# The first layer's gate and second scale vectors on TensorE: two more modulation vectors as column-tiled products with c

## The chip, the core and the metric

The kernel runs on one core of a Trainium2 chip. The core has a matrix engine (TensorE, PE in the profile; its weight loads are listed as PEld), a vector engine (VectorE, DVE), a scalar engine for activations and copies (ScalarE, ACT), a general engine (GpSimd, POOL) and a queue from which the transfers from memory are issued (SyncE, SP). They run side by side, each through its own instructions in order, and wait for one another through semaphores. The metric is the device time of one execution in microseconds; lower is better.

## The reference

Four residual layers over 256 tokens of width 1024; the mixers are sliding-window attention, gated linear attention, forgetting attention and sliding-window attention again. Every layer has six modulation vectors, made from one conditioning vector `c`:

```python
c_act = jax.nn.silu(c)
for i in range(DEPTH):
    mod = c_act @ ada_w[i] + ada_b[i]                 # (1, 1024) @ (1024, 6144)
    sh1, sc1, g1, sh2, sc2, g2 = jnp.split(mod, 6, axis=-1)
    h = modulate(rmsnorm(x, norm_gain[i, 0]), sh1, sc1)
    y = mixer_i(h)                                    # layer 0: swa_mixer
    x = x + g1[:, None, :] * y
    h = modulate(rmsnorm(x, norm_gain[i, 1]), sh2, sc2)
    x = x + g2[:, None, :] * swiglu(h, ffn_w_gu[i], ffn_w_down[i])
return rmsnorm(x, final_norm)
```

`modulate(h, shift, scale)` is `h * (1 + scale) + shift`. The vectors are numbered 0 to 5 in the order of the split. Everything is float32. `ada_w` alone is 4 x 6 x 4 MB, and all weights are read once: 296 MB in one execution.

## The kernel before

All weights come as a stream of items of at most 1 MB, kept in order by the class `Stream`. An item is loaded into one of five `raw` buffers (`RAW = 5`) on SP's queue (`load_raw`, L181), so the load of an item waits until the item five places earlier is done with its buffer. There are two kinds of items.

A weight item ("w") is split into a high and a low part for the three-product matmul `mm3` (L277 to L279): ACT makes `wh` (L194) and DVE subtracts to make `wl` (L196), in two pieces each.

A modulation item ("a") holds the weights of 256 entries of one modulation vector. Before the change there are two ways to use it. For most vectors `ada_pieces` gives two pieces, each a DVE instruction over 128 x 1024 elements that multiplies the weights by `cact` (c after silu, on every partition) and sums (L213); it writes one column of 128 entries of `mod`. For the first two vectors of layer 0 (shift and scale of the first norm) `ada_rows` gives a product and a turn instead. The product is eight matmuls with a 32-column `ccol` as stationary operand and 256 columns of weights moving, which go to four groups of 32 columns of the array and so to four groups of partitions of one PSUM bank (L228), followed by an ACT copy to `row` (L229). The turn is two matmuls of `row` with a column of ones, which adds the four groups and turns the row into two columns (L233), and a DVE add of the bias into `mod` (L235). For these vectors the weights lie in memory by rows of `c`, 256 columns to an item (`_layout`).

In layer 0 the order of items is written out by hand in `ORDER0 = "shwshshwshwwwgwwgggSwHSwHSSHHw"`: w is the next weight item of the mixer (six input chunks i0_0 to i0_5, four output chunks o0_0 to o0_3), and s, h, g, H, S are the next item of vectors 1, 0, 2, 3, 4, four of each. The pieces of the items are put into the program between the matmuls of the chunks: `start_chunk` divides the pieces pending (up to two weight items ahead) by the eight ticks of a chunk, and each `tick` emits as many as are due. A tick comes after six matmuls of `mm3`. The same tick advances the attention, which runs as a generator (`attn_heads`) between the projections: scores (L576), masked minimum on DVE (L589), exponentials on ACT (L594), scaling (L562, L564), transposes (L617, copied at L618), the product with v (L606), and the split of the result (L510, L511). The chunks of q are rotated on DVE (L639 to L646) and transposed (L679).

`out_proj` then forces the gate (vector 2) and multiplies in two halves of the inner dimension; each output tile is added to x with the gate on DVE (L514). Before the second half `next_norm` forces vectors 3 and 4 (H and S). The PSUM tag "mm" has three banks, which hold the results of the projections; "t" has two and holds transposes, statistics and the results of `ada_rows`. The instructions of an engine don't stand strictly in program order: in the trace the attention's matmuls are found between those of a projection.

Of the kernel before, what the change touches and what calls it, by code (L numbers as in the profile page):

```python
# [17 lines left out]
P = 128  # L18
D = 1024
KT = D // P  # L20
S = 256
# [46 lines left out]
GLA_RATE = (0.585, 2.55)  # L68
FOX_RATE = (0.64, -7.0, 0.68, 1.02)
STAT = (1, 1, 1)  # L70
PSBUFS = {"mm": 3, "s": 2, "t": 2, "o": 1}


# [69 lines left out]
class Builder:  # L143
# [24 lines left out]
    def ps(self, tag):  # L168
        return self.t(self.psum, [P, 512], tag, bufs=PSBUFS[tag])

# [29 lines left out]
    def ada_pieces(self, it, raw):  # L200

        nc = self.nc
        layer, nt = it[1]
        mod = self.mod[layer]
        bias = self.c("ada_b")[:, layer * 48:(layer + 1) * 48]

        if layer == 0 and nt < 2 * KT:
            return self.ada_rows(mod[:, nt:nt + 2], bias[:, nt:nt + 2], raw)

        def piece(i):  # L210
            w = raw[:, i * D:(i + 1) * D]
            col, b = mod[:, nt + i:nt + i + 1], bias[:, nt + i:nt + i + 1]
            nc.vector.tensor_tensor_reduce(out=w, in0=w, in1=self.cact, scale=1.0, scalar=b,  # L213
                                           op0=ALU.mult, op1=ALU.add, accum_out=col)
        return [lambda: piece(0), lambda: piece(1)]

    def ada_rows(self, mod, bias, raw):


        nc = self.nc  # L220
        w = raw[:, :2048].rearrange("p (k n) -> p k n", k=KT)
        ps = self.ps("t")
        row = self.t(self.small, [P, S], "fc", bufs=2)

        def product():
            for k in range(KT):
                j = k % 4 * 32
                nc.tensor.matmul(ps[j:j + 32, :S], self.ccol[:, k], w[:, k], start=k < 4, stop=k >= 4)  # L228
            nc.scalar.copy(row, ps[:, :S])  # L229

        def turn():
            for m in range(2):
                nc.tensor.matmul(ps[:, S + m:S + m + 1], row[:, m * P:(m + 1) * P], self.c("one"),  # L233
                                 start=True, stop=True)
            nc.vector.tensor_tensor(out=mod, in0=ps[:, S:S + 2], in1=bias, op=ALU.add)  # L235
        return [product, lambda: self.turns.append(turn)]


    def start_chunk(self, ticks):
# [224 lines left out]
    def first_chunk(self, name, tok=False):  # L464
# [9 lines left out]
        for k in range(KT):  # L474
            for m in range(2):
                sl = slice(m * P, (m + 1) * P)
                first, last = k == 0, k == KT - 1
                self.mm3(outs[m][:, :S + 2], wh[:, k, sl], wl[:, k, sl], uh[:, k], ul[:, k], first, last)
            if k == STAT[0]:
                self.stat_start(self.acc)  # L480
            if k == STAT[1]:
                self.stat_end()
            if k == STAT[2]:
                nc.scalar.copy(rbs, self.spread(self.y))
# [811 lines left out]
def _chunks(w, cols):  # L1296

    k, n = w.shape
    return w.reshape(k // P, P, n // cols, cols).transpose(2, 1, 0, 3).reshape(n // cols, P, -1)


def _halves(w):

    n = w.shape[0]
    return w.reshape(n, 2, 4, P, 2, 512).transpose(0, 1, 4, 3, 2, 5).reshape(n, 4, P, 2048)


def _colmajor(v):

    return v.reshape(-1, P).T  # L1310


def _layout(i):
    f = np.float32
    a = {}
    a["x"] = i["x"][0].T.reshape(KT, P, S).transpose(1, 0, 2)
    a["c"] = i["c"].reshape(1, D)
    ada = i["ada_w"].reshape(DEPTH, D, 6, D).transpose(0, 2, 3, 1)
    a["ada"] = ada.reshape(DEPTH * 6, 4, 2, P, D).transpose(0, 1, 3, 2, 4).reshape(DEPTH * 6, 4, P, 2 * D)
    for v in range(2):  # L1320
        a["ada"][v] = _chunks(i["ada_w"][0, :, v * D:(v + 1) * D], 256)
    gu = i["ffn_w_gu"].reshape(DEPTH, KT, P, 2, FT, P)[:, :, :, :, :2]
    gu = gu.transpose(0, 4, 2, 1, 3, 5).reshape(DEPTH, 2, P, KT * 2 * P)
    gt = i["ffn_w_gu"].reshape(DEPTH, 2, KT // 2, P, 2, FT // 2, 2 * P)[:, :, :, :, :, 1:]
    gt = gt.transpose(0, 5, 1, 3, 2, 4, 6).reshape(DEPTH, FT - 2, P, KT * 2 * P)
    a["gu"] = np.concatenate([gu, gt], 1)
    dn = i["ffn_w_down"].reshape(DEPTH, 2, FT // 2, P, KT, P)
    a["down"] = dn.transpose(0, 4, 1, 3, 2, 5).reshape(DEPTH, KT, 2, P, (FT // 2) * P)

    swa = i["swa_w_in"]  # L1330
    a["swa_in"] = np.stack([_chunks(np.concatenate([w[:, 1024:], w[:, :1024]], 1), 256) for w in swa])
    a["swa_o"] = _halves(i["swa_w_o"])
    w = i["gla_w_in"][0]
    gq, gk, gv, gr, ga = np.split(w, [512, 1024, 2048, 3072], axis=1)
    a["gla_in"] = _chunks(np.concatenate(
        [gr, gq[:, :256], gk[:, :256], gq[:, 256:], gk[:, 256:], gv], 1), 256)[None]
    a["gla_va"] = _chunks(np.concatenate([gv[:, :256], ga], 1), 272)[0]
    a["gla_gate"] = i["gla_w_gate_up"][0]
    a["gla_o"] = _halves(i["gla_w_o"])
    w = i["fox_w_in"][0]  # L1340
    fq, fk, fv, ff = np.split(w, [1024, 2048, 3072], axis=1)
    a["fox_in"] = _chunks(np.concatenate(
        [t[:, 256 * g:256 * g + 256] for g in range(4) for t in (fq, fk, fv)], 1), 256)[None]
    a["fox_vf"] = _chunks(np.concatenate([fv[:, :256], ff], 1), 272)[0]
    a["fox_o"] = _halves(i["fox_w_o"])

    c, c2 = np.zeros((P, CONST_W), f), np.zeros((P, CONST2_W), f)

    def put(name, v):
        lo, hi = COFF[name] if name in COFF else C2OFF[name]  # L1350
        (c if name in COFF else c2)[:v.shape[0], lo:hi] = v
    put("ident", np.eye(P, dtype=f))
    put("ones", np.tile(np.array([[1.0 / D, 1.0 / 256]], f), (P, 1)))
    put("one", np.ones((P, 1), f))
    put("c", _colmajor(i["c"]))
    put("eps", np.full((P, 1), EPS, f))
    put("gain", _colmajor(i["norm_gain"]))
    put("ada_b", _colmajor(i["ada_b"]))
    put("fin", _colmajor(i["final_norm"]))
    put("hnorm", _colmajor(i["gla_head_norm"][0]))  # L1360
    put("bgate", _colmajor(i["gla_b_gate"][0]))
    put("sinks", np.tile(i["swa_sinks"].reshape(1, 32), (P, 1)))
    put("bf", i["fox_b_f"].reshape(16, 1))
    inv = (f(1.0) / (f(150000.0) ** (np.arange(0, HD, 2, dtype=f) / f(HD)))).astype(f)
    ang = (np.arange(S, dtype=f)[:, None] * inv[None, :]).astype(f)
    cos, sin = np.cos(ang).astype(f), np.sin(ang).astype(f)
    tok = lambda t: t.reshape(NB, P, HD).transpose(1, 0, 2).reshape(P, NB * HD)
    put("cos", tok(np.concatenate([cos, cos], 1)))
    put("sin", tok(np.concatenate([-sin, sin], 1)))
    qi, kj = np.arange(P)[:, None], np.arange(P)[None, :]  # L1370
    off = lambda ok: np.where(ok, f(0), f(BIG)).astype(f)
    caus, full = off(kj <= qi), np.zeros((P, P), f)
    put("swamask", np.concatenate([caus, off(kj > qi), caus], 1))
    put("foxmask", np.concatenate([caus, full, caus], 1))
    put("scan", np.tile((np.arange(S) % 64 != 0).astype(f)[None], (P, 1)))
    a["const"] = c
    a["const2"] = c2
    s, t = np.arange(P)[:, None], np.arange(P)[None, :]
    a["gla_masks"] = np.stack(
        [((s // (2 * B) == t // (2 * B)) & ((s // B) % 2 == 0) & ((t // B) % 2 == 1))  # L1380
         for B in LEVELS + (64,)], 1).astype(np.int32)
    return {k: np.ascontiguousarray(v) for k, v in a.items()}
# [18 lines left out]
```

## Time and profile before

| | |
|---|---|
| median of three runs | 1260.54 us (1259.45 to 1266.03) |
| profiled execution | 1260.51 us, span 1258.7 us |
| PE busy | 1207.7 us, 96% of the span |
| DVE busy | 1000.2 us, 79% |
| ACT busy | 698.3 us, 55% |
| POOL busy | 136.3 us, 11% |
| first layer's mixer up to the first half of its output projection | 0 to 139.3 us of the span |
| read from memory | 296 MB, 236 GB/s over the span |

The span runs from the first to the last instruction; the time of an execution is slightly longer. Busy shares are averages over stages with different limits, and a matmul's duration overlaps with the next one's, so PE's busy time is more than its work: what counts for PE is the step from one matmul to the next. In the profile's lists a row gives start, duration, engine, line and operation, then the tile written and the tiles read, then in brackets the idle time before it and what ended that. The chain of waits follows the work that ended last back from the end, and lists its pieces in order of time.

### The profile page before, as it was taken

The page shows a single profiled execution, that of the slowest core. Times are in us where ns is not written, and L with a number is a line of the kernel's source. Part 1 is how long each engine was busy: PE and PEld are TensorE (multiplying, and loading weights), DVE is VectorE, ACT ScalarE, POOL GpSimd, SP SyncE. Part 2 cuts the span into 40 slices and gives each one's busy share as a digit, 9 for nine tenths or more (in the row PEclk, how much of TensorE's full clock was granted, in tenths as well). Part 3 has the DMA queues.
Part 4 walks back from the last instruction along what each step waited for, and adds up shares of the span by engine and source line. Part 5 has one row for each costly group of instructions (what it writes and reads, how often), then busy time and mean ns, then how long its engine had stood idle before and what let it go on. Part 6 is the DMA issues. An engine that isn't in the chain of part 4 may idle for free.

```text
span 1258.7 us, 19761 instructions
## 1 busy us (share of the span) xinstructions
PE 1207.7 (96%) x7444; PEld 1053.3 (84%) x7444; DVE 1000.2 (79%) x1826; ACT 698.3 (55%) x1294; POOL 136.3 (11%) x177
## 2 busy tenths in 40 slices
PE   5898799999998999999999999999999999999997
PEld 3786788888888998888889999888888979888886
DVE  2598998888779989988878758988888998766553
ACT  3475564444486756444557867544445677544442
POOL 0011110001104412000011101100011011000011
PEclk8898899999999999999999999999999999999999
DMA  8655779977745445988875543699788444665440
GB/s 358 250 220 203 271 282 364 336 284 260 280 148 183 147 141 204 363 323 306 274 281 214 206 174 135 250 349 339 281 274 281 168 164 168 215 220 211 162 162 34
DMA packets 44673, 298.51 MB, mean 237 GB/s; under 512 B 5169, under 2 KB 5329, under 8 KB 14242
## 3 DMA queue, kind: packets, MB, share of 16 engines
q1 hardware_dynamic: 43778, 295.54, 64.9%
q8 instruction: 58, 0.95, 0.3%
q10 hardware_dynamic: 432, 1.20, 0.2%
q0 software_dynamic: 368, 0.53, 0.1%
q14 instruction: 37, 0.30, 0.1%
HBM read 296.16 MB, written 1.05 MB: 236 GB/s over the span
## 4 chain that ended last, share of the span: by engine, by line
PE 84%; DVE 7%; ACT 4%; issue 2%; DMA 2%; POOL 1%; DVEq 0%; SPq 0%; ACTq 0%; POOLq 0%
PE mm L1133 13%; PE mm L277 12%; PE mm L278 11%; PE mm L279 11%; PE s L278 7%; PE s L277 7%; PE s L279 7%; PE mm L1135 7%; PE s L576 2%; DVE wl L196 2%; PE o L606 2%; DVE raw L213 1%; PE t L1104 1%; PE t L617 1%; ACT wh L194 1%
## 5 line engine op out<-in xcount | busy, mean ns | idle before, releaser
L196 DVE TENSOR_TENSOR wl<-raw,wh 128x1024 fp32r<-128x1024 f32 (+2 forms) x408 | 447.2, 1129 | 88.0 <-ACT wh L194 86.9
L194 ACT CAST wh<-raw 128x1024 fp32r<-128x1024 f32 (+2 forms) x408 | 376.2, 964 | 230.7 <-issue 108.8
L1133 PE MATMUL mm<-a,wh 128*128 128x512 f32 x704 | 247.8, 396 | 0.0
L213 DVE CUSTOM_DVE_ANT_0 raw<-raw,cact,const 128x1024 f32<-128x1024 f32 x176 | 224.1, 1292 | 11.2 <-DMA raw<-in_ada 11.1
L277 PE MATMUL mm<-wh,hh 128*128 128x512 f32 (+1 forms) x560 | 198.8, 356 | 6.1 <-ACT hh L454 5.8
L1135 PE MATMUL mm<-a,wl 128*128 128x256 f32 x704 | 197.6, 281 | 0.0
L278 PE MATMUL mm<-wl,hh 128*128 128x512 f32 (+1 forms) x560 | 194.5, 348 | 0.2 <-DVE wl L196 0.2
L279 PE MATMUL mm<-wh,hl 128*128 128x512 f32 (+1 forms) x560 | 193.5, 347 | 0.0
L1133 PEld LDWEIGHTS mm<-a,wh 128*128 128x128 f32 x704 | 132.2, 188 | 30.4
L277 PE MATMUL s<-wh,hh 128*128 128x512 f32 (+2 forms) x384 | 145.1, 379 | 2.9 <-ACT hh L454 2.9
L278 PE MATMUL s<-wl,hh 128*128 128x512 f32 (+2 forms) x384 | 143.6, 375 | 0.6 <-DVE wl L196 0.6
L279 PE MATMUL s<-wh,hl 128*128 128x512 f32 (+2 forms) x384 | 142.1, 374 | 0.0
L433 POOL TENSOR_TENSOR sq<-sq,sq 128x256 f32<-128x256 f32 x48 | 53.9, 1123 | 758.4 <-ACT sq L422 732.2
L1135 PEld LDWEIGHTS mm<-a,wl 128*128 128x128 f32 x704 | 132.6, 188 | 0.2
L277 PEld LDWEIGHTS mm<-wh,hh 128*128 128x128 f32 x560 | 107.0, 191 | 21.3 <-ACT hh L454 6.2
L278 PEld LDWEIGHTS mm<-wl,hh 128*128 128x128 f32 x560 | 107.1, 192 | 12.8 <-issue 0.7
L279 PEld LDWEIGHTS mm<-wh,hl 128*128 128x128 f32 x560 | 106.9, 192 | 13.0 <-issue 0.2
L514 DVE SCALAR_TENSOR_TENSOR x<-mm,mod,x 128x256 f32<-128x256 f32 x128 | 61.5, 481 | 44.7 <-PE mm L1135 37.5
L277 PEld LDWEIGHTS s<-wh,hh 128*128 128x128 f32 x384 | 72.5, 189 | 15.5 <-ACT hh L454 3.4
L278 PEld LDWEIGHTS s<-wl,hh 128*128 128x128 f32 x384 | 72.8, 190 | 12.6 <-DVE wl L196 0.8
L279 PEld LDWEIGHTS s<-wh,hl 128*128 128x128 f32 x384 | 72.2, 190 | 13.1
L277 PE MATMUL mm<-oh,wh 128*128 128x256 f32 x256 | 74.8, 297 | 8.3 <-DVE x L514 8.2
(218 smaller groups left out, 2007.8 us busy)
## 6 DMA issues: line engine op xcount, KB each, us to landing
raw<-in_ada SPq DMA_DIRECT2D x96, 1024.0 KB, 6.3
raw<-in_gu SPq DMA_DIRECT2D x88, 1024.0 KB, 5.6
raw<-in_down SPq DMA_DIRECT2D x64, 704.0 KB, 4.7
raw<-in_swa_in SPq DMA_DIRECT2D x12, 1024.0 KB, 5.3
raw<-in_gla_in SPq DMA_DIRECT2D x11, 1024.0 KB, 4.9
raw<-in_fox_in SPq DMA_DIRECT2D x11, 1024.0 KB, 6.0
raw<-in_swa_o SPq DMA_DIRECT2D x8, 1024.0 KB, 5.0
raw<-in_gla_o SPq DMA_DIRECT2D x4, 1024.0 KB, 4.8
```

The costliest lines, as they stand in the source:

```text
L194: nc.scalar.copy(wh[:, sl], raw[:, sl])
L196: eng.tensor_tensor(out=wl[:, sl], in0=raw[:, sl], in1=wh[:, sl].bitcast(F32), op=ALU.subtract)
L213: nc.vector.tensor_tensor_reduce(out=w, in0=w, in1=self.cact, scale=1.0, scalar=b, op0=ALU.mult, op1=ALU.add, accum_out=col)
L277: nc.tensor.matmul(out, ah, bh, start=first, stop=False)
L278: nc.tensor.matmul(out, ah, bl, start=False, stop=False)
L279: nc.tensor.matmul(out, al, bh, start=False, stop=last)
L433: (eng or nc.gpsimd).tensor_tensor(out=q, in0=self.acc, in1=q, op=ALU.add)
L514: self.nc.vector.scalar_tensor_tensor(out=self.x[:, m], in0=ps, scalar=gate[:, m:m + 1], in1=self.x[:, m], op0=ALU.mult, op1=ALU.add)
L576: nc.tensor.matmul(sc[:, so:s1], q[:, so:so + P], k[:, :k1], start=True, stop=True)
L606: nc.tensor.matmul(o[rows, b * P:S], vs[e][b], pt[:, e, :S] if b == 0 else pt[:, e, S:], start=b == 0, stop=b == 1)
L1133: nc.tensor.matmul(o, wh[:, k], a[:, kk].rearrange("p e n -> p (e n)"), start=kk == 0, stop=False)
L1135: nc.tensor.matmul(o[:, S:], wl[:, k], a[:, kk, 0], start=False, stop=kk == FT - 1)
```

## The change

The set of layer 0's vectors that go through `ada_rows` grows from {0, 1} to {0, 1, 2, 4}: the gate of the mixer (g) and the scale of the second norm (S) are added; the shift of the second norm (H) and the gate of the feed-forward layer stay on DVE. The weights of the two vectors are laid out by rows of c like those of the first two, with the same number of items and bytes. The bank and the `row` tile are now taken when the product is emitted. For vectors 0 and 1 (`early`) the bank is of tag "t" and the turn is put on a list, as before; for 2 and 4 the bank is of tag "mm" and the turn is the item's second piece, emitted when the next piece is due.

```diff
+ROWS = (0, 1, 2, 4)
...
-        if layer == 0 and nt < 2 * KT:
-            return self.ada_rows(mod[:, nt:nt + 2], bias[:, nt:nt + 2], raw)
+        if layer == 0 and nt // KT in ROWS:
+            return self.ada_rows(mod[:, nt:nt + 2], bias[:, nt:nt + 2], raw, nt < 2 * KT)
...
-    def ada_rows(self, mod, bias, raw):
+    def ada_rows(self, mod, bias, raw, early):
         nc = self.nc
         w = raw[:, :2048].rearrange("p (k n) -> p k n", k=KT)
-        ps = self.ps("t")
-        row = self.t(self.small, [P, S], "fc", bufs=2)
+        ps = row = None
         def product():
+            nonlocal ps, row
+            ps = self.ps("t" if early else "mm")
+            row = self.t(self.small, [P, S], "fc", bufs=2)
             for k in range(KT):
                 j = k % 4 * 32
                 nc.tensor.matmul(ps[j:j + 32, :S], self.ccol[:, k], w[:, k], start=k < 4, stop=k >= 4)
             nc.scalar.copy(row, ps[:, :S])
         def turn():
             for m in range(2):
                 nc.tensor.matmul(ps[:, S + m:S + m + 1], row[:, m * P:(m + 1) * P], self.c("one"),
                                  start=True, stop=True)
             nc.vector.tensor_tensor(out=mod, in0=ps[:, S:S + 2], in1=bias, op=ALU.add)
-        return [product, lambda: self.turns.append(turn)]
+        return [product, (lambda: self.turns.append(turn)) if early else turn]
...
-    for v in range(2):
+    for v in ROWS:
         a["ada"][v] = _chunks(i["ada_w"][0, :, v * D:(v + 1) * D], 256)
```

## The prediction

> **What bounds the kernel now.** I read the page first, then the windows, then the chain that ended last, then the timelines of TensorE (PE), VectorE (DVE) and ScalarE (ACT).
>
> ```profile
> span 1258.7 us, 19761 instructions
> ```
>
> The profiled execution took 1260.51 us: its span and 1.8 us around it. That is 0.03 us from the median of the three runs (1260.54), so I subtract from 1260.5. Only the first layer's mixer is touched. I cut it by what PE works on: input chunks (64 to 92.4), attention and the first half of the output projection (to 123.3), the rest of that half (to 139.3).
>
> ```profile
> core 0: us, PE busy (x) PEld busy (x) DVE busy (x) ACT busy (x) POOL busy (x), PEclk, DMA share, GB/s
> 64.00:92.40 28.40, 28.08 (x230) 24.06 (x230) 27.11 (x86) 20.96 (x59) 5.76 (x16) 1.00 0.55 202
> 92.40:123.30 30.90, 26.61 (x171) 19.45 (x170) 26.98 (x80) 18.25 (x59) 5.80 (x12) 0.89 0.57 204
> 123.30:139.30 16.00, 7.81 (x49) 6.92 (x48) 16.00 (x29) 5.58 (x7) 0.00 (x0) 0.89 0.92 349
> 64.00:139.30 75.30, 62.50 (x446) 50.43 (x445) 70.09 (x192) 44.79 (x124) 11.57 (x28) 0.93 0.64 234
> ```
>
> DVE is busy for 70.09 of 75.30 us, and in the last stretch for all of it, while PE stands half idle there. In the first stretch both are full. The chain of waits says what DVE does:
>
> ```profile
> 89.35 1.19 DVE raw L213
> ...
> 96.12 1.20 DVE raw L213
> ...
> 123.38 1.19 DVE raw L213
> ...
> 135.41 1.19 DVE raw L213
> 136.61 2.27 DVE wl L196 x2
> 138.88 0.41 DVE x L514
> 139.33 0.39 PE mm L277
> ```
>
> The product-and-sum of the modulation vectors (L213) is on the path that sets the end: five between 89.35 and 97.3, ten between 123.4 and 136.6. In program order the 24 pieces of this stretch are eight of the gate (g), then S and H interleaved; the first five on the chain are g, g, g, S, S, and of the ten last four are S and six H. So 9 of the 16 pieces that go lie on the chain, 10.8 us at 1.20.
>
> ```profile
> L213 DVE CUSTOM_DVE_ANT_0 raw<-raw,cact,const 128x1024 f32<-128x1024 f32 x24 | 30.0, 1282 | 0.0
> 101.78 0.43 DVE L639 TENSOR_TENSOR r<-mm,const 128x256 f32<-128x256 f32 x1
> 92.05 0.28 PE L279 MATMUL mm<-wh,hl 128*128 128x256 f32 x1
> 103.41 0.45 PE L679 MATMUL t<-const,qr 128*128 128x128 f32 x1 [3.22 <-ACT wh L194]
> ```
>
> PE issued the last matmul of chunk i0_5 at 92.05; DVE came to rotate its result (L639) at 101.78, over 9 us late, and PE stood still before the transpose that needs it (L679, 3.22 us; the engine named is ACT, but what it transposes is DVE's).
>
> **What goes.** Four items of g and four of S, two pieces each: 16 pieces. A piece lasts 1.28 us, but the next starts 1.20 us after it (chain rows), so DVE loses 16 x 1.20 = 19.2 us.
>
> **What comes.** Each item becomes a product (eight matmuls, 16 records), an ACT copy, a turn (two matmuls, four records) and a DVE add. The first stage already does this for the vectors h and s:
>
> ```profile
> 46.93 1.86 PE t L228 x32
> 48.79 0.55 PE t L233 x4
> 49.43 0.16 DVE L235 TENSOR_TENSOR mod<-t,const 128x2 f32<-128x2 f32 x1 [5.76 <-PE t L233]
> 48.91 0.37 ACT L229 COPY fc<-t 128x256 f32<-128x256 f32 x1 [0.49 <-PE t L228]
> 46.65 0.28 PE L279 MATMUL s<-wh,hl 128*128 128x256 f32 x1
> 46.86 1.93 PE L228 MATMUL t<-raw,ccol 128*32 128x256 f32 x32
> 83.07 0.38 PE L277 MATMUL mm<-wh,hh 128*128 128x256 f32 x1
> 83.29 0.28 PE L278 MATMUL mm<-wl,hh 128*128 128x256 f32 x1
> 60.01 0.12 PE mm L278
> ```
>
> Two products took 1.86, so one is 0.93; a turn 0.55. Changing between kinds of product costs about 0.1 each time: 0.21 from a mixer product to the first L228 where the usual step is 0.12, and 0.22 instead of 0.12 after an attention product. With entry and exit of the product (0.19) and the turn's exit (0.10) an item costs PE 1.77 us, eight 14.2. A product between mixer products is shown nowhere; below it stands 0 (it falls wholly into PE's waits), above it 1.77 plus an uncovered wait of the turn. The adds are 8 x 0.16 = 1.3 us of DVE, the copies 8 x 0.37 = 3.0 of ACT, which is busy for 44.8 of 75.3: I cost both at nothing, since DVE falls to 70.1 - 19.2 + 1.3 = 52.2.
>
> The Trainium skill, page "TensorEngine Tiling (Array Packing)", section Key Properties, says that a change of tiling mode drains TensorE, which speaks against putting column tiles between full products. If each of the 16 changes waited out the rest of a 0.28 us matmul beyond its 0.12 step, that estimate is 2.6 us where I count 1.5, and the sum would be 1256.6. The rows above show 0.09 and 0.10 for a change, less than that wait.
>
> **The turn's wait.** It needs the ACT copy, and PE works in order, so all mixer products behind it wait with it.
>
> ```profile
> 34.70 1.17 PE t L228 x16
> 35.95 0.38 ACT fc L229
> 36.37 0.61 PE t L233 x4
> 97.78 0.69 ACT L562 ACTIVATE pr<-pr,rd 128x128 f32<-128x128 f32 x2 [2.45 <-DVE rd L560]
> ```
>
> Uncovered, it is 0.5 us (35.87 to 36.37), 4.0 for eight; if the copy also stands behind an ACT instruction that waits for DVE, up to 2.45 more. In program order most turns are one tick later than their product, with six mixer products (0.7 us) between. I take nothing, nearer to the first row, and keep both ends. The product takes one of three "mm" banks until its add: 0 if one is free, and up to two H pieces (2.4 us) for each of two S products in the output projection if the bank hangs on L514 behind them. I take 0: PE has enough other work.
>
> **What moves.** No DMA is added; an item is 1024 KB as before. Its buffer comes free when PE has read it, not DVE, and SP's queue loads the item five later then. That is earlier or equal, since DVE was the late one. The last output weights (o0_3) wait for an H item as before. In the last stretch, at 349 GB/s, there is the least room; its products need items loaded earlier.
>
> **PE's own time**, since PE becomes the fullest:
>
> ```profile
> L576 PE MATMUL s<-uh,qT 64*128 64x128 f32 (+1 forms) x64 | 10.0, 377 | 0.0
> L606 PE MATMUL o<-pt,v 128*64 128x256 f32 (+1 forms) x64 | 9.6, 365 | 1.1 <-DVE rd L560 1.1
> L617 PE MATMUL t<-const,pr 128*128 128x128 f32 x48 | 7.2, 276 | 0.3 <-ACT pr L562 0.3
> L679 PE MATMUL t<-const,qr 128*128 128x128 f32 x16 | 3.2, 318 | 3.2 <-ACT wh L194 3.2
> 82.28 0.86 PE s L576 x8
> 84.04 0.80 PE o L606 x8
> 86.24 0.66 PE t L617 x6
> 88.57 0.44 PE t L679 x4
> ```
>
> Of 446 records 192 are attention; 254 at 0.12 are 30.5. Attention: 8 x 0.86 + 8 x 0.80 + 8 x 0.66 + 4 x 0.44 = 20.3. Changes from these 28 groups back to mixer products (8 + 8 + 8 + 4) at 0.1 add 2.8. Together 53.6 of 75.3; 21.7 are waiting and slow clock. After: 53.6 + 14.2 = 67.8, so 7.5 us can be won at most if PE bounds. I leave these waits: 0.3 in the first stretch (28.40 less 28.08), 1.4 of attention (the L606 and L617 rows), and 2.2 in the last stretch, where DVE keeps the lead: six H pieces 7.2, four L514 at 0.41, two L196 2.3, adds 0.3, together 11.4, against PE's 48 x 0.12 + 2 x 1.77 = 9.3. 7.5 - 3.9 = 3.6.
>
> ```profile
> 139.30:145.00 5.70, 5.67 (x35) 5.67 (x36) 5.20 (x10) 3.11 (x7) 0.73 (x1) 0.70 0.78 302
> 141.14 0.21 PE mm L277
> ```
>
> After PE's idle stretch the granted clock is 0.70, and some 16 matmuls step by 0.21 instead of 0.12. With PE kept busy that is 16 x 0.09 = 1.4 more (bounds 0 and 1.4). Forecast: 1260.5 - 3.6 - 1.4 = **1255.5 us**. Behind it the feed-forward layer is PE's and starts that much earlier.
>
> **Rivals.** (a) *The products fall into PE's waits.* For: 21.7 us of them, against 14.2. Against: the first stretch, where five of eight items are due, has none. Then the chain loses its 10.8: 1249.7. (b) *Given back.* The five items lengthen the full first stretch by 8.9; in return only DVE's lag goes (101.78 - 92.17 = 9.6), and the last stretch keeps its length since the S products wait for banks behind H: 1260.5 - 0.7 = 1259.8. For: both engines are full up to 92.4. Against: six H pieces can't fill 16 us. (c) *Slower: turns behind ACT's queue.* If six of eight turns meet a wait like that at 97.78, PE stands 14.7 us: 1255.5 + 14.7 = 1270.2. It outweighs the gain from 5.0 / 8 = 0.6 us a turn, and shows beyond 0.5% from 1.4. Against: those ACT waits came from DVE's lag, which shrinks. That the change does not take place can't be: the test on ROWS takes vectors 2 and 4 of layer 0 alone.
>
> **Chances.** A measurement of this kernel can tell about 0.5%, 6.3 us, from no change: faster is below 1254.2, slower above 1266.8. Forecast 0.55 (1252 to 1259; 0.22 of it below 1254.2), (a) 0.20, (b) 0.13, (c) 0.12. Faster 0.42, within 0.46, slower 0.12. The range runs from (a), a little below it, to beyond (b) and the forecast with its uncovered turns (1255.5 + 4.0 + 2.4): 1249 to 1262; (c) is left out.
>
> **What would show it.** Right: L213 eight times instead of 24 in the mixer, DVE near 52 us there; the i0_5 rotation starts within 2 us of PE's last matmul; PE's waits before L277 for L514 (6.0) halved; the clock after the mixer near 1. Wrong: PE idle before L233 for ACT over 0.6 us each (c), idle before L228 for a bank (b), or the input chunks not lengthened at all (a). A DMA wait before a product would break the sum too.

## The result and the profile after

Twenty executions of each kernel, side by side on the same chip:

| | median, us | lowest to highest |
|---|---|---|
| before | 1263.99 | 1257.61 to 1272.07 |
| after | 1256.63 | 1249.96 to 1259.94 |

The ratio is 0.9937 with a 95% interval of 0.9924 to 0.9950: 6 to 10 us less, 7.4 by the medians.

The two profiled executions differ by only 1.9 us (1260.51 and 1258.57), and the reason has to be seen before they are compared. In both, PE issues the same matmuls up to the first product of the gate (at 69.12 in the later profile). Yet the first rotation of keys, ahead of that product, starts 5.6 us later in the profile of after. Here are VectorE's timelines (start, duration, engine, line, operation), before first, then after; the code of after is three lines longer from there on, so L639 became L642.

```profile
52.71 0.42 DVE L639 TENSOR_TENSOR r<-mm,const 128x256 f32<-128x256 f32 x1 [0.87 <-PE mm L279]
...
154.67 0.17 DVE L343 RECIPROCAL y<-sd 128x2 f32<-128x2 f32 x1 [0.15 <-ACT sd L342]
```

```profile
58.33 0.42 DVE L642 TENSOR_TENSOR r<-mm,const 128x256 f32<-128x256 f32 x1 [0.63 <-PE mm L282]
...
153.25 0.17 DVE L346 RECIPROCAL y<-sd 128x2 f32<-128x2 f32 x1
```

Two things are to be seen: what lies ahead of the change differs between two executions by nearly as much as the change is worth, and from that first rotation to the second norm's reciprocal (the mixer from here on) the kernel before took 101.96 us and the one after 94.92. That is 7.04 us less, close to the medians. Behind the mixer the two profiles differ by 0.5 us. A second profile of the changed kernel (e12 below) began at 55.50 and took 94.90, so its length repeats to 0.02 us where the start does not; of the kernel before, and of each variant, there is one profile. All profiles below are compared by the length of the mixer, cut in four: **I** up to the rotation of the last input chunk, **II** up to the last split of an attention result, **III** up to the eighth add to x, the last of the first half of the output projection, **IV** up to the reciprocal. The windows of after, and those of before at the same cuts:

```profile
58.33:107.62 49.29, 48.47 (x430) 39.42 (x428) 38.81 (x118) 34.03 (x89) 6.33 (x20) 1.00 0.67 256
107.62:129.30 21.68, 21.55 (x153) 15.19 (x150) 15.96 (x52) 14.02 (x45) 2.15 (x8) 1.00 0.50 190
129.30:138.41 9.11, 9.11 (x91) 7.68 (x91) 7.80 (x14) 4.79 (x8) 0.00 (x0) 1.00 0.65 254
138.41:153.25 14.84, 14.46 (x121) 14.15 (x121) 14.36 (x26) 11.09 (x24) 7.14 (x6) 1.00 0.82 328
58.33:153.25 94.92, 93.58 (x787) 76.44 (x786) 76.94 (x208) 63.93 (x163) 15.62 (x34) 1.00 0.65 252
```

```profile
52.71:101.78 49.07, 45.82 (x356) 40.01 (x355) 47.25 (x130) 34.29 (x92) 10.59 (x22) 0.97 0.63 232
101.78:122.95 21.17, 19.54 (x120) 13.93 (x121) 17.25 (x52) 11.54 (x35) 0.98 (x7) 0.84 0.46 154
122.95:138.80 15.85, 8.16 (x52) 7.27 (x51) 15.85 (x26) 5.58 (x7) 0.00 (x0) 0.89 0.91 342
138.80:154.67 15.87, 14.74 (x109) 14.53 (x110) 14.90 (x25) 10.47 (x22) 5.28 (x6) 0.89 0.61 228
52.71:154.67 101.96, 88.25 (x635) 75.73 (x635) 95.25 (x231) 61.88 (x155) 16.85 (x34) 0.92 0.63 232
```

After the length come the busy times of PE, PEld, DVE, ACT and POOL, the granted clock, the share of the DMA engines and GB/s. DVE fell from 95.25 of 101.96 to 76.94 of 94.92; PE rose from 88.25 to 93.58, all but 1.34 us of the mixer, and its clock to 1.00. The bound has changed hands. And the time did not come from all over: I and II are 0.2 and 0.5 us longer than before, III is 6.7 shorter, IV 1.0.

The groups of after that answer to those of before (line, engine, operation, tile; busy time and mean ns; idle time before and its cause):

```profile
L214 DVE CUSTOM_DVE_ANT_0 raw<-raw,cact,const 128x1024 f32<-128x1024 f32 x8 | 10.2, 1274 | 0.0
L231 PE MATMUL mm<-raw,ccol 128*32 128x256 f32 x128 | 9.8, 386 | 0.0
L236 PE MATMUL mm<-const,fc 128*128 128x1 f32 x32 | 4.2, 237 | 0.0
L280 PE MATMUL mm<-oh,wh 128*128 128x256 f32 x64 | 18.6, 293 | 0.0
```

Eight pieces are left on DVE, eight products and turns came to PE, and neither they nor the output projection (L280) wait for anything. Before, the same group of the output projection stood idle for VectorE's add to x:

```profile
L277 PE MATMUL mm<-oh,wh 128*128 128x256 f32 x64 | 20.0, 315 | 8.2 <-DVE x L514 8.2
```

### The profile page after: what moved, and what is told of

The parts are those of the page before. It is cut to its first block, busy times and chain, and to the rows that moved or that the text cites. A ratio compares the mean times of both kernels' runs of the same rounds, so it can differ in the third digit from the quotient of the medians.

```text
span 1256.8 us, 20072 instructions
## 1 busy us (share of the span) xinstructions
PE 1218.5 (97%) x7604; PEld 1059.3 (84%) x7604; DVE 981.9 (78%) x1802; ACT 700.8 (56%) x1302; POOL 135.2 (11%) x177
## 4 chain that ended last, share of the span: by engine, by line
PE 86%; DVE 6%; ACT 3%; issue 2%; DMA 2%; POOL 1%; DVEq 0%; SPq 0%; ACTq 0%; POOLq 0%
PE mm L1136 13%; PE mm L280 12%; PE mm L281 12%; PE mm L282 11%; PE s L280 7%; PE s L281 7%; PE s L282 7%; PE mm L1138 7%; PE s L579 2%; DVE wl L197 2%; PE o L609 2%; PE t L1107 1%; PE t L620 1%; ACT wh L195 1%; PE t L231 1%
## 5 line engine op out<-in xcount | busy, mean ns | idle before, releaser
L214 DVE CUSTOM_DVE_ANT_0 raw<-raw,cact,const 128x1024 f32<-128x1024 f32 x160 | 204.4, 1294 | 16.0 <-DMA raw<-in_ada 15.9
L280 PE MATMUL mm<-wh,hh 128*128 128x512 f32 (+1 forms) x560 | 199.7, 357 | 5.7 <-ACT hh L457 5.5
L280 PE MATMUL s<-wh,hh 128*128 128x512 f32 (+2 forms) x384 | 145.4, 380 | 2.9 <-ACT hh L457 2.9
L280 PEld LDWEIGHTS mm<-wh,hh 128*128 128x128 f32 x560 | 107.4, 192 | 22.0 <-ACT hh L457 5.9
L280 PEld LDWEIGHTS s<-wh,hh 128*128 128x128 f32 x384 | 72.8, 190 | 15.5 <-ACT hh L457 3.4
L282 PEld LDWEIGHTS s<-wh,hl 128*128 128x128 f32 x384 | 72.3, 190 | 13.1
L281 PE MATMUL mm<-ol,wh 128*128 128x256 f32 x256 | 73.6, 288 | 0.0
```

The lines of the kernel that those rows point to most:

```text
L280: nc.tensor.matmul(out, ah, bh, start=first, stop=False)
L281: nc.tensor.matmul(out, ah, bl, start=False, stop=False)
L282: nc.tensor.matmul(out, al, bh, start=False, stop=last)
```

## The experiments

Times are set against the kernel before on the same chip (medians 1264.32, 1263.99 and 1263.18 us for e1 to e4, e5 to e8 and e9 to e12); the mixer and its cuts come from each run's profile. Where an expectation is set against the changed kernel, the run's ratio is compared with 0.9937 (in e9 to e12 with e12's).

| run | ratio [95%] | mixer | I | II | III | IV |
|---|---|---|---|---|---|---|
| before | 1 | 101.96 | 49.07 | 21.17 | 15.85 | 15.87 |
| after | 0.9937 [0.9924, 0.9950] | 94.92 | 49.29 | 21.68 | 9.11 | 14.84 |
| e1 neither | 0.9827 [0.9800, 0.9854] | 83.60 | 42.16 | 18.45 | 7.01 | 15.98 |
| e2 both engines | 1.0017 [0.9999, 1.0034] | 107.40 | 54.24 | 19.63 | 17.37 | 16.16 |
| e3 gate only | 0.9942 [0.9921, 0.9962] | 95.63 | 48.73 | 18.34 | 12.23 | 16.33 |
| e4 scale only | 0.9942 [0.9921, 0.9962] | 95.31 | 48.19 | 19.58 | 12.73 | 14.81 |
| e5 products twice | 0.9965 [0.9945, 0.9984] | 100.08 | 54.18 | 20.28 | 9.17 | 16.45 |
| e6 second shift too | 1.0022 [1.0002, 1.0042] | 102.33 | 49.33 | 20.70 | 15.99 | 16.31 |
| e7 turn at once | 0.9958 [0.9941, 0.9975] | 97.93 | 52.23 | 21.54 | 9.32 | 14.84 |
| e8 bank of tag t | 0.9958 [0.9934, 0.9982] | 97.24 | 50.38 | 21.04 | 9.50 | 16.32 |
| e9 second gate too | 0.9988 [0.9966, 1.0011] | 95.41 | 49.80 | 21.67 | 9.11 | 14.83 |
| e10 six items | 0.9960 [0.9942, 0.9977] | 99.39 | 49.31 | 21.68 | 12.22 | 16.18 |
| e11 split on POOL | 0.9977 [0.9958, 0.9997] | 99.29 | 51.84 | 20.98 | 11.67 | 14.80 |
| e12 after again | 0.9933 [0.9909, 0.9956] | 94.90 | 49.28 | 21.67 | 9.12 | 14.83 |

### e1 and e2: one engine at a time

**e1** takes the 16 pieces off DVE and gives PE nothing; the products of the two vectors are left out.

```diff
+        if layer == 0 and nt // KT in (2, 4):
+            return [lambda: nc.vector.tensor_tensor(out=mod[:, nt:nt + 2], in0=raw[:, :2],
+                                                    in1=bias[:, nt:nt + 2], op=ALU.add),
+                    lambda: None]
```

> Leaves out the products of the gate and the second scale of layer 0: each item is only a small DVE add of its first two columns to the bias (0.16 us), so DVE is relieved as by the change, and PE and ACT get nothing. Theory 1 (the items are no longer free on PE: what the change wins behind the last attention pair, about 7 us, is net of some 8 to 9 us that five products cost the full input chunks): 14 to 17 us under before. Rival (PE's items fall into its waits, only DVE counted): 7 to 9 us under before, like the change.

Measured: 18.5 to 25.3 us under before (18.36 less in the mixer), beyond both ranges and nearer to theory 1's. **e2** keeps the 16 pieces on DVE and does the products, copies and turns besides.

```diff
-ROWS = (0, 1, 2, 4)
+ROWS = (0, 1)
...
+                    nc.tensor.matmul(ps[j:j + 32, :S], self.ccol[:, k],
+                                     self.cact[:, k % 4 * S:(k % 4 + 1) * S], start=k < 4, stop=k >= 4)
...
+            return [lambda: (piece(0), product()), lambda: (piece(1), turn())]
```

> DVE keeps its 16 pieces for the two vectors, and PE and ACT do eight products, copies and turns besides, on a constant tile, with no add behind them. Theory 1: the input chunks (64 to 92 us) are full on PE, so five items there cost 1.5 to 1.8 us each: 6 to 10 us over before; the three S items behind them fall into waits for DVE. Rival (they fall into waits everywhere): 0 to 3 us over before.

Measured: 0.1 under to 4.3 over before; 5.44 us longer in the mixer, of which 5.17 in stage I. Together with before and after they make a square:

| mixer, us | PE without the items | PE with them |
|---|---|---|
| DVE with its 16 pieces | 101.96 (before) | 107.40 (e2) |
| DVE without | 83.60 (e1) | 94.92 (after) |

Taking the pieces from DVE is worth 18.4 us, about what the 16 pieces take there (16 x 1.20 less eight small adds, 17.9) and more than the nine that the chain of waits showed. The granted clock may have a part in it: before, stages II to IV ran at 0.84 and 0.89, in e1 at 1.00. How the 18.4 divides between the pieces and the clock is not shown. The eight items on PE cost 5.4 us beside a full DVE, but 11.3 beside a relieved one. The change nets 18.4 - 11.3. The rival of e1 (PE's items free) is out. In e2 theory 1's 6 to 10 us were missed. Five items cost 5.2 in stage I, a little less than it said, and the other three were hidden, as it said (0.3 more behind stage I). The total moved less than the mixer, about into the rival's range. In the profile e2 began its mixer at 50.64, 2.1 us earlier than before did; whether its other executions did so is not recorded.

### e3 and e4: one vector at a time

```diff
-ROWS = (0, 1, 2, 4)
+ROWS = (0, 1, 2)
```

> Only the gate (vector 2) goes to PE, the second scale stays on DVE. Theory 1 (relief of DVE up to the last attention pair is paid back by PE, and only DVE work behind that pair counts): within 1.5 us of before. Rival (the lag of DVE at the rotation of the last input chunk, 9.6 us before, is what counted): 4 to 6 us under before.

> Only the second scale (vector 4) goes to PE, the gate stays on DVE. Theory 1: most or all of the gain, 5 to 8 us under before, since four of its pieces and the H pieces behind them stood after the last attention pair. Rival (lag at the rotation): 2 to 3 us under before.

(e4 has `ROWS = (0, 1, 4)`.) Both measured 4.8 to 10.0 us under before, and 6.3 and 6.7 less in the mixer. For e4 theory 1 was right; for e3 it was wrong, and the rival was nearer, though the point it named did not move (stage I is only 0.3 shorter). The gate's pieces stand ahead of the last attention pair, and yet their going shortened II by 2.8 and III by 3.6. DVE takes up its remaining pieces earlier when it has room: ten of them began in stage III before, seven in e3, and three pieces are 3.6 us. DVE still fills that stage in e3, at a clock of 0.89:

```profile
123.17:135.40 12.23, 7.87 (x57) 7.17 (x55) 12.23 (x23) 5.69 (x7) 0.00 (x0) 0.89 0.93 355
```

Four items give nearly all that eight give.

### e5 and e6: more for PE

e5 issues each late product twice; e6 puts the second shift there too.

```diff
-            for k in range(KT):
+            for k in [*range(KT)] * (1 if early else 2):
```

> The changed kernel with the eight matmuls of each late product issued twice (the second pass starts the sums anew), so PE gets 8 x 1.0 us more and nothing else changes. Theory 2 (formed after e1 to e4: before, DVE filled the mixer; after, PE does, with no room left): all of it shows, 7 to 9 us over the changed kernel, so about as long as before. Rival (DVE or the attention's latency still sets parts of the mixer): 2 to 4 us over the changed kernel.

```diff
-ROWS = (0, 1, 2, 4)
+ROWS = (0, 1, 2, 3, 4)
```

> The second shift (vector 3) goes to PE too: twelve items there, none of the mixer's on DVE. Theory 2 (PE is the bound with eight): 4 x 1.5 to 1.8 us more, 5 to 8 us over the changed kernel, though DVE loses eight pieces more. Rival (DVE still leads behind the last attention pair, six H pieces there): 2 to 5 us under the changed kernel.

e6: the mixer is 7.4 us longer than after, back at before's length; that is 1.85 us for each further item. The ratio lies 0.85% over after's, 10.7 us and beyond theory 2's range. The direction is theory 2's, and the rival is out. Stage III of e6 shows it bare:

```profile
123.80:139.79 15.99, 15.99 (x162) 11.99 (x162) 5.48 (x15) 5.81 (x10) 0.00 (x0) 1.00 0.74 260
```

Before, this stage was DVE's for its whole 15.85 us; here it is PE's for 15.99, with DVE down to 5.48. In e5 the mixer grew by 5.2 us, and the ratio lies 0.28% over after's, 3.5 us. Theory 2 expected 7 to 9 and was missed, the rival 2 to 4: PE sets a good part of the mixer, not all of it.

### e7 and e8: the turn's wait and the bank

```diff
-        return [product, (lambda: self.turns.append(turn)) if early else turn]
+        if not early:
+            return [lambda: (product(), turn()), lambda: None]
+        return [product, lambda: self.turns.append(turn)]
```

> The turn of each late item is put into the program right behind its product, instead of at the next due piece. If the wait for the ACT copy is uncovered then, PE stands 0.5 us or more in eight places: 3 to 6 us over the changed kernel. If other matmuls are put between all the same, or the wait costs nothing: within 1.5 us of the changed kernel.

```diff
-            ps = self.ps("t" if early else "mm")
+            ps = self.ps("t")
```

> The late products take a bank of tag t (two banks, shared with the transposes) instead of mm (three, shared with the projections). If banks of mm hold the output projection back in the changed kernel: 1 to 4 us under it. If the transposes of the attention need both t banks: 1 to 5 us over it. If banks don't matter: within 1 us.

e7 measured 0.21% (2.7 us) over the changed kernel in ratio, the two intervals overlapping; its mixer is 3.0 longer, 2.9 in stage I, where the granted clock was 0.97 against 1.00. Of that PE stood still before the turns for only 0.5 us, in one place and not in eight:

```profile
L236 PE MATMUL mm<-const,fc 128*128 128x1 f32 x32 | 4.5, 246 | 0.5 <-ACT fc L232 0.5
```

In the changed kernel it is 0.0 (the row above). So a tick's distance covers the wait, and without it the wait is small. How the rest of the 3.0 divides between clock and order stays open; e9, whose stage I has after's instructions and also a clock of 0.97, is only 0.5 longer there. e8 gained nothing: its ratio is that of e7, and the mixer was 2.3 longer, most of it in IV (1.5) and I (1.1). By this and by the 0.0 idle before L231 and L280 above, banks of tag mm don't hold the changed kernel back.

### e9: the price of an item where nothing hides it

```diff
-ROWS = (0, 1, 2, 4)
+ROWS = (0, 1, 2, 4, 5)
```

> The gate of layer 0's feed-forward layer (vector 5) goes to PE as well: four more items, between the products of the gate-and-up stage, where PE has no idle time already and DVE has room. This prices an item where nothing hides it. Theory 2 (an item costs PE 1.4 to 1.9 us, as e6 showed): 5.5 to 7.5 us over the changed kernel. Rival (products slip between weight loads and cost less): under 3 us.

The four items fall into the feed-forward stage. From the mixer's end to the ninth group's transposes (L1107, in the chain of waits) after took 267.61 - 153.25 = 114.36 us, e9 269.69 - 148.54 = 121.15: 6.8 more, **1.70 an item**. By the ratios beside the same before (0.9988 and 0.9933) it is 0.55%, 6.9 us. The rival is out. In the changed kernel one item's steps read off PE's timeline:

```profile
68.91 0.28 PE L282 MATMUL mm<-wh,hl 128*128 128x256 f32 x1
69.12 1.07 PE L231 MATMUL mm<-raw,ccol 128*32 128x256 f32 x16
70.12 0.39 PE L280 MATMUL mm<-wh,hh 128*128 128x256 f32 x1
70.34 0.28 PE L281 MATMUL mm<-wl,hh 128*128 128x256 f32 x1
...
71.65 0.50 PE L236 MATMUL mm<-const,fc 128*128 128x1 f32 x4
72.01 0.36 PE L280 MATMUL mm<-wh,hh 128*128 128x256 f32 x1
72.22 0.28 PE L281 MATMUL mm<-wl,hh 128*128 128x256 f32 x1
```

From start to start: 1.00 for the product and 0.36 for the turn, and the steps around them are 0.21, 0.22 and 0.21 where 0.12 is usual, 0.28 more: 1.64 us.

### e10 to e12: a better split?

e10 leaves the last two scale items on DVE; e11 has the scale alone on PE and half of each weight split on POOL; e12 is the changed kernel.

```diff
-        if layer == 0 and nt // KT in ROWS:
+        if layer == 0 and nt // KT in ROWS and nt < 4 * KT + 4:
```

> Six items go to PE: all four of the gate and the first two of the second scale; the other two stay on DVE. Theory 2 (PE sets the mixer with eight items, DVE with none, and with four the two are even): between e3 or e4 and the changed kernel or a little under both, 7 to 10 us under before. Rival (which engine has the item matters less than where it stands; the last two scale items on DVE delay the end): 4 to 6 us under before.

```diff
-MIX_POOL = ((), (), (), ())
+MIX_POOL = ((1,), (), (), ())
```

> Only the second scale on PE (as e4), and the second half of each weight split of layer 0's mixer chunks moves from DVE to POOL, so that both PE and DVE have less. If e4 is held by DVE and PE together: up to 5 us under e4. If POOL's split (4 us or more by its 1.1 us for a quarter of the elements) comes late for PE: over e4, up to before's time.

> The changed kernel once more on the same chip and beside the same runs of before, so that six items and the price of an item can be set against it: 5 to 9 us under before by every theory.

e10's stages I and II are those of the changed kernel to 0.03 us; then the two items tell:

```profile
127.03:139.25 12.22, 9.40 (x69) 8.91 (x68) 12.22 (x20) 5.54 (x7) 0.00 (x0) 0.88 0.78 278
139.25:155.43 16.18, 14.89 (x109) 14.47 (x110) 14.56 (x26) 10.48 (x22) 5.26 (x6) 0.88 0.60 224
```

```profile
126.45:135.57 9.12, 9.12 (x91) 7.69 (x91) 7.80 (x15) 4.80 (x8) 0.00 (x0) 1.00 0.65 253
135.57:150.40 14.83, 14.44 (x121) 14.13 (x121) 14.37 (x25) 11.09 (x24) 7.15 (x6) 1.00 0.82 328
```

With two S items on DVE (above) it is busy for all of stage III, PE stands still for 2.8 us, and the clock is 0.88 into stage IV; with them on PE (e12, below) PE is busy throughout at clock 1.00. Moving these last two items makes 4.5 of the 7.0 us of the mixer (by the ratios, whose intervals overlap, 3.4 us of the whole). The rival of e10 was right with its 4 to 6 us under before (5.1 measured): where an item stands counts. Set against e3, which has all four scale items on DVE, e10 is even 3.8 us longer in the mixer. Its first two scale items cost 0.6 in I and 3.3 in II and took nothing off III (12.22 and 12.23, with seven pieces begun there in both). e11 is slower than e4, 4.0 us in the mixer: its stage I is 3.7 us longer, with POOL's busy time in it up from 6.3 to 23.9 us and DVE's up from 45.2 to 48.2. No version here that does all the work beats the changed kernel. Only the last two scale items on PE, all others staying on DVE, was not tried.

## Why the prediction was right

The forecast named the right mechanism and made the gain a third too small: 5.0 us, where 7.4 (6 to 10) were measured. That 1255.5 lies only 1.1 us from 1256.63 is luck, since the kernel before measured 1263.99 beside it, 3.5 us more than the 1260.5 that the forecast subtracts from.

**The bound and its change of hands** held. PE's idle for L514 was forecast to halve and went; the rotation of i0_5 starts 0.9 us after PE's last product of that chunk (106.74 to 107.62) instead of over 9; the clock in 139.3 to 145 is 1.00; DVE does eight pieces, not 24, and no product waited for a DMA. DVE in 64 to 139.3, forecast at 52, was 57.55, since that window of the later profile holds more of the mixer's beginning; over stages I to III it fell by 17.8 us (80.35 to 62.57), where 17.9 was forecast.

**"Nine of the 16 pieces lie on the chain, 10.8 us"** was too little as a measure of what DVE held back: e1 shows 18.4, clock included. The chain names one path at a time; in stage I, where both engines were full, it named five pieces at the end (three of the gate), and relieving DVE alone shortened that stage by 6.9 us. The forecast did not rest on it but on PE's own time.

**The item's price**, 1.77 us, is 1.64 by the steps in place and 1.70 by e9. What was costed at nothing (ACT's copies, the turn's wait, the banks) cost nothing that the profile shows: idle before L231 and L236 is 0.0. The Trainium skill, page "TensorEngine Tiling (Array Packing)", section Key Properties, has a mode change drain TensorE. In this trace the steps into and out of a product are 0.09 and 0.10 us longer than usual, less than the 0.16 that the rest of a 0.28 us matmul would take.

**The step that was off** is a term of the sum: "I leave these waits", 3.9 us, and in it the 2.2 for the last stretch, where DVE was to keep the lead with 11.4 us of work against PE's 9.3 (the difference is 2.1). It lasted 9.11 us, PE-bound throughout. The forecast kept all six H pieces in that stretch; three were done there, the others earlier:

```profile
116.22 1.28 DVE L214 CUSTOM_DVE_ANT_0 raw<-raw,cact,const 128x1024 f32<-128x1024 f32 x1
...
120.44 1.27 DVE L214 CUSTOM_DVE_ANT_0 raw<-raw,cact,const 128x1024 f32<-128x1024 f32 x1
...
126.60 1.28 DVE L214 CUSTOM_DVE_ANT_0 raw<-raw,cact,const 128x1024 f32<-128x1024 f32 x1
...
129.64 1.27 DVE L214 CUSTOM_DVE_ANT_0 raw<-raw,cact,const 128x1024 f32<-128x1024 f32 x1
...
131.24 1.27 DVE L214 CUSTOM_DVE_ANT_0 raw<-raw,cact,const 128x1024 f32<-128x1024 f32 x1
...
133.85 1.28 DVE L214 CUSTOM_DVE_ANT_0 raw<-raw,cact,const 128x1024 f32<-128x1024 f32 x1
```

Stage III began at 129.30. By its parts the forecast takes 4.6 us off the last stretch (16.0 to 11.4), which leaves 1.0 us of loss for the two stretches ahead, and 1.4 off what follows; measured were 6.7, 0.7 and 1.0. Without the 2.2 us the sum is 3.6 + 2.2 + 1.4 = 7.2, against 7.04 in the mixer. That it fits so well is in part luck: with the item's measured price of 1.64 it would be 8.2.

**The rivals.** (a), products hidden in PE's waits, is out: of eight items' 13.1 us (at 1.64) 11.3 show. (b), given back, was right for stage I (five items there, and it is 0.2 longer; e1 takes 6.9 off, e2 puts 5.2 on) and wrong for the last stretch. (c), turns behind ACT's queue, did not happen.

## What to carry to other kernels

When work moves from a full engine to the next fullest, neither what it took there nor what it takes here is the gain: a kernel with it on neither engine and one with it on both show the two terms, here 18.4 and 11.3 us, and how much room is left. The chain of waits gave less than that here (10.8 us) for a load on an engine that was full beside another full one. And it matters where the moved piece stands: the two items in the stage where the old engine was full and the new one half idle made 4.5 of 7.0 us, while the two ahead of them, moved alone beside the gate, made the mixer 3.8 us longer.

## What the hardware showed that was not expected

The same instructions ahead of the mixer took from 50.6 to 58.3 us in these profiles (e11, which changes the splits there, left out). The granted clock in 20 to 40 us goes with it. Where it was 0.84 or more, the mixer began at 50.6 to 51.8; at 0.66 to 0.74, at 52.7 to 53.8; at 0.56 to 0.59, at 55.5 to 58.3. The rows below are those of after, of before and of e1, whose mixers began at 58.33, 52.71 and 50.81.

```profile
20.00:40.00 20.00, 14.62 (x84) 9.77 (x84) 6.50 (x16) 4.07 (x9) 1.02 (x4) 0.56 0.72 269
```

```profile
20.00:40.00 20.00, 13.64 (x105) 9.32 (x105) 7.89 (x22) 4.81 (x11) 1.02 (x4) 0.74 0.82 313
```

```profile
20.00:40.00 20.00, 13.59 (x118) 9.87 (x118) 9.29 (x24) 6.67 (x13) 1.02 (x4) 1.00 0.92 349
```

In this start PE is busy for about 14 of 20 us, and the mean clock differs from execution to execution, with up to 7.7 us of difference in where the mixer begins. That the clock alone makes it is not shown: the bytes moved in that window mostly go with it too (269 to 349 GB/s in these rows). A change worth 7 us is seen in single profiles only between two events that both lie behind such a stretch.
